# The product PA of the state space on GpSimd, its fin sums with it, and a small copy on ScalarE

## The chip, the cores and the metric

The kernel runs on one core of a Trainium2 chip. The metric is the device time of one execution in microseconds; three executions of the kernel before took 2797.89, 2802.87 and 2807.26 us, so its median is 2802.87. The engines are TensorE (PE in the rows, PEld its weight loads), VectorE (DVE), ScalarE (ACT), GpSimd (POOL) and the queue that issues the transfers (SP).

## The reference, cut to what matters

The reference is one step of a two-layer backbone: attention and an MLP in layer 0, a bidirectional S5 (a state space with 64 groups of 16 channels and a complex diagonal state of 64) with a GLU and an MLP in layer 1. The change touches the state space alone:

```python
def _ssm_scan(u, lam_re, lam_im, log_dt, b_re, b_im, s0_re, s0_im, reverse):
    ...
    bu_re = jnp.einsum('blgc,gpc->blgp', u, bb_re)
    bu_im = jnp.einsum('blgc,gpc->blgp', u, bb_im)
    ...
    _, _, s_re, s_im = lax.associative_scan(_complex_affine_combine, (a_re, a_im, bu_re, bu_im), axis=1)
    ...

def _bidir_s5(h, s0, lam_re, ..., d_skip, w_a, w_b):
    ...
    for d in range(2):
        s_re, s_im = _ssm_scan(u, ..., reverse=(d == 1))
        y = (y + jnp.einsum('blgp,gcp->blgc', s_re, c_re[d])
             - jnp.einsum('blgp,gcp->blgc', s_im, c_im[d]))
        states.append((s_re, s_im))
    y = jax.nn.gelu(y.reshape(b, l, D_MODEL).astype(h.dtype))
    return (y @ w_a) * jax.nn.sigmoid(y @ w_b), states
```

The last states of the context tokens are an output of their own.

## The kernel before, in words

The state space (function s5) works on chunks of 8 tokens: 145 columns stand for the chunks of both streams and a gap between them. The 64 groups go in 16 batches of GB = 4; the partitions hold the 64 states of the forward scan (lo) and the 64 of the backward scan (hi). A complex scan becomes two real ones, one for the real and one for the imaginary part (k = 0, 1), since each state is turned by its angle before the scan and turned back after it; D holds the cosines and sines of the turns.

For one batch b the steps are these:
- v_mm: 32 small products on TensorE write V in PSUM, one buffer (L1068).
- scan(b): ScalarE makes the decay factors `at` (L1078) and copies the initial states into W (L1081); GpSimd clears one column of W (L1082). VectorE turns V: four products of D, in SBUF, with V, in PSUM, into W and t (L1087, L1089), which are called rotations below, then a sum and a difference of W and t, both in SBUF (L1092), called the two sums. It copies the initial states of the backward scan into one column of W (L1094) and runs two scans over `at` and W into Zs (L1098). ScalarE copies Zs into Z, the backward half reversed (L1101, L1102), and GpSimd clears one column of Z (L1103).
- states(b): VectorE turns back: PA, the product of the cosines and Z for both parts at once, 2 x 4 x 146 elements per partition (L1112), and PB, the product of the sines and Z with a sign, in two instructions (L1114). Two sums of 4-element columns of PA and PB give `fin`, the last states (L1117).
- t_mm and y_mm: TensorE adds what the chunk gives to itself (L1127) and 32 products of PA and PB with the matrices ex (L1137) in PSUM; ScalarE copies the sum out (L1140).
- out_y, after each second batch: transfers rearrange the result, and ScalarE makes the GELU (L1153).

W, t, Zs, Z, PA and PB have one buffer each, `at` has two. The loop calls scan(b), then v_mm and t_mm for batch b + 1, then states(b - 1) and y_mm(b - 1). All waits are set by the framework, which also orders each engine's instructions: by the order of the program as priority, among those whose inputs and buffers are ready in its own model of time. So the order on an engine is fixed when the kernel is built and isn't that of the program: in the trace PA of batch b - 1 stands between the sums and the scans of batch b.

In the first batches GpSimd also forms the products of x and rb for the inputs u (L1034 in load_u), from which ScalarE makes hs (L1038). Behind the state space come the splits of y and of the GLU's weights (L52) and the GLU's matmuls.

Of the kernel before, what the change touches and what calls it, by code (L numbers as in the profile page):

```python
# [13 lines left out]
ALU = mybir.AluOpType  # L14
# [5 lines left out]
D = 1024  # L20
# [13 lines left out]
class Body:  # L34
# [746 lines left out]
    NT = 147  # L781
# [119 lines left out]
    GB = 4  # L901
# [100 lines left out]
    def s5(self):  # L1002
        if isinstance(self.YD, int):
            self.YD = YS[self.YD]; self.UD = YS[self.UD]
        nc, tc, a, GB, ND, NT = self.nc, self.tc, self.a, self.GB, self.NT, self.NT - 1
        v, gp, act = nc.vector, nc.gpsimd, nc.scalar
# [11 lines left out]
        with ExitStack() as c2:  # L1018
# [51 lines left out]
                               start=q % 2 == 0, stop=q % 2 == 1, skip_group_check=True)  # L1070
                return V

            def scan(b, V, D):

                gsl = slice(GB * b, GB * b + GB)
                at = S.tile([128, GB, NT], F32, name="at", tag="at", bufs=2)
                for q in range(GB):
                    act.activation(at[:, q, :], am[:, 0:NT], AF.Copy, scale=self.zs[:, GB * b + q, 2:3])  # L1078
                W = S.tile([128, 2, GB, NT], F32, name="W", tag="W", bufs=1)
                zin = self.zs[:, gsl, 0:2].rearrange("p g k -> p k g")  # L1080
                act.copy(W[lo, :, :, 0], zin[lo])  # L1081
                gp.memset(W[hi, :, :, 0:1], 0.0)  # L1082
                t = S.tile([128, 2, GB, 145], F32, name="t", tag="t", bufs=1)
                for k in range(2):
                    vk = [V[:, j, :, 0:290].rearrange("p a (g k) -> p a g k", k=145) for j in (k, 1 - k)]
                    d = [D[:, :, j, 2:147].rearrange("p (a g) k -> p a g k", a=2) for j in range(2)]
                    v.tensor_tensor(out=W[:, k, :, 1:146].rearrange("p (a g) k -> p a g k", a=2), in0=d[0],  # L1087
                                    in1=vk[0], op=ALU.mult)
                    v.tensor_tensor(out=t[:, k].rearrange("p (a g) k -> p a g k", a=2), in0=d[1], in1=vk[1],  # L1089
                                    op=ALU.mult)  # L1090
                for k in range(2):
                    v.tensor_tensor(out=W[:, k, :, 1:146], in0=W[:, k, :, 1:146], in1=t[:, k],  # L1092
                                    op=ALU.add if k == 0 else ALU.subtract)
                v.tensor_copy(W[hi, :, :, 17], zin[hi])  # L1094
                Zs = S.tile([128, 2, GB, NT], F32, name="Zs", tag="Zs", bufs=1)
                for k in range(2):
                    af, wf, zf = (z.rearrange("p g i -> p (g i)") for z in (at, W[:, k], Zs[:, k]))
                    v.tensor_tensor_scan(out=zf, data0=af, data1=wf, initial=0.0, op0=ALU.mult, op1=ALU.add)  # L1098
                Z = S.tile([128, 2, GB, NT], F32, name="Z", tag="Z", bufs=1)
                with self.tc.high_priority(offset=self.HZ):  # L1100
                    act.copy(Z[hi, :, :, 0:145], Zs[hi, :, :, 144::-1])  # L1101
                    act.copy(Z[lo], Zs[lo])  # L1102
                gp.memset(Z[hi, :, :, 145:146], 0.0)  # L1103
                return Z

            def states(b, Z, D):

                gsl = slice(GB * b, GB * b + GB)
                PA = S.tile([128, 2, GB, NT], F32, name="PA", tag="PA", bufs=1)
                PB = S.tile([128, 2, GB, NT], F32, name="PB", tag="PB", bufs=1)  # L1110
                d_r, d_i = D[:, :, 0, 1:147], D[:, :, 1, 1:147]
                v.tensor_tensor(out=PA, in0=d_r[:, None].to_broadcast([128, 2, GB, NT]), in1=Z, op=ALU.mult)  # L1112
                for k in range(2):
                    v.scalar_tensor_tensor(out=PB[:, k], in0=d_i, scalar=am[:, NT + k:NT + k + 1], in1=Z[:, 1 - k],  # L1114
                                           op0=ALU.mult, op1=ALU.mult)
                for r, c in ((lo, 145), (hi, 128)):
                    v.tensor_tensor(out=self.fin[r, :, gsl], in0=PA[r, :, :, c], in1=PB[r, :, :, c], op=ALU.add)  # L1117
                return PA, PB

            def t_mm(b, u, bt):  # L1120

                out = []
                for g in range(0, GB, 2):
                    yp = ps.tile([128, 512], F32, name="yp", tag="y", bufs=2) if b % 2 == 0 else self.bank("yp")
                    out.append(yp)
                    for q in (g, g + 1):
                        mm(yp[:, 145 * (q - g):145 * (q - g) + 145], bt[:, q, 256:384], u[:, GB * (b % 2) + q, :],  # L1127
                           start=q == g, stop=False, skip_group_check=True)
                return out

            def y_mm(b, yps, ex, PA, PB, y8):
                for g, yp in zip(range(0, GB, 2), yps):
                    for q in (g, g + 1):
                        o = yp[:, 145 * (q - g):145 * (q - g) + 145]
                        for k in range(2):
                            for P in (PA, PB):
                                mm(o, ex[:, q, k, :], P[:, k, q, 0:145], start=False, stop=k == 1 and P is PB,  # L1137
                                   skip_group_check=True)
                    gq = GB * (b % 2) + g
                    act.copy(y8[:, gq:gq + 2, :], yp[:, 0:290].rearrange("p (g k) -> p g k", k=145))  # L1140
# [20 lines left out]
            for b in range(nb + 1):  # L1161
                if b < nb:
                    if b == 0:
                        us[1] = load_u(1)
                    if b % 2 == self.LU and (b + self.LU) // 2 + 1 < KT and b:
                        with self.tc.high_priority(offset=self.HU):
                            us[(b + self.LU) // 2 + 1] = load_u((b + self.LU) // 2 + 1)
                    if b + 1 < nb:
                        with self.tc.high_priority(offset=self.HT):
                            tb[b + 1] = load_t(b + 1)  # L1170
                    Zs[b] = scan(b, Vs.pop(b), tb[b][1])
                    if b + 1 < nb:
                        Vs[b + 1] = v_mm(b + 1, us[(b + 1) // 2], tb[b + 1][0])
                        Ts[b + 1] = t_mm(b + 1, us[(b + 1) // 2], tb[b + 1][0])
                if b > 0:
                    c = b - 1
                    if c % 2 == 0:
                        y8 = S.tile([128, 8, 145], F32, name="y8", tag="y8", bufs=1)
                    y_mm(c, Ts.pop(c), tb[c][2], *states(c, Zs.pop(c), tb[c][1]), y8)
                    if c == nb - 1:  # L1180
                        self.gw0 = [self.glu_w(k, 0) for k in range(2)]
                    if c % 2 == 1:
                        out_y(c // 2, y8)
# [216 lines left out]
```

## Time and profile before

| | before |
|---|---|
| three executions, median | 2802.87 us |
| the profiled execution, its own time | 2799.74 us |
| its span, first to last instruction | 2797.8 us |
| mean granted TensorE clock | 0.979 of 2.4 GHz |
| busy: TensorE, VectorE, ScalarE, GpSimd | 93%, 65%, 39%, 13% of the span |
| the state space | about 1568 to 1745 us |

The profile is one execution, read by the chip's profiler. Shares of busy time are means over stages with different limits, so a stage has to be cut out to see what bounds it there. A row of the timeline gives the start, the duration, the engine, the line, the operation, what it writes and reads, the shape and how many instructions are merged in it; in brackets stands the idle time of the engine ahead of it and what ended that. VectorE's records overlap a little: the distance between two starts is what an instruction costs the queue.

### The profile page before, as it was taken

What the parts mean: (1) busy time and instruction counts of PE and PEld (TensorE: products, weight loads), DVE (VectorE), ACT (ScalarE), POOL (GpSimd) and SP (SyncE); (2) the same over time, 40 slices, a digit from 0 to 9 for tenths busy, and PEclk for the clock granted to TensorE, in tenths of its full rate; (3) what the DMA queues carried; (4) which work ended last, traced back from release to release, by engine and by line L of the source; (5) the groups of instructions that cost most, each with busy time, mean ns of one, the idle gap of its engine ahead of it and who ended that gap; (6) DMA issues with size and microseconds to landing.
All of it is one profiled execution on the core that took longest, in us unless ns stands there. A gap on an engine that the chain in (4) does not pass through costs nothing. (4 is left out here: it accounts for less than half of the span.)

```text
span 2797.8 us, 44016 instructions
## 1 busy us (share of the span) xinstructions
PE 2609.5 (93%) x16561; PEld 2462.1 (88%) x16561; DVE 1824.4 (65%) x4342; ACT 1096.1 (39%) x2295; POOL 366.6 (13%) x476
## 2 busy tenths in 40 slices
PE   6889999998899999999899687999999999999997
PEld 4767987886699989899899676999999999999997
DVE  4847777785576787887875799545645354454455
ACT  3545666662223323332333655434422222212224
POOL 1222222210022132121220400000000000000002
PEclk8999999999999999999999799999999999999998
DMA  7353222235532233132223586433110111111101
GB/s 264 109 169 105 84 79 74 81 116 189 180 103 75 70 95 90 55 105 71 88 83 91 174 251 180 141 121 113 46 46 31 46 46 46 34 43 46 46 31 68
DMA packets 128452, 271.67 MB, mean 97 GB/s; under 512 B 13296, under 2 KB 67952, under 8 KB 126832
## 3 DMA queue, kind: packets, MB, share of 16 engines
q1 hardware_dynamic: 128240, 268.86, 30.3%
q8 instruction: 131, 2.15, 0.3%
q14 instruction: 81, 0.66, 0.1%
HBM read 214.22 MB, written 39.81 MB: 91 GB/s over the span
## 5 line engine op out<-in xcount | busy, mean ns | idle before, releaser
L455 DVE SCALAR_TENSOR_TENSOR x<-m,mod,x 128x384 f32<-128x384 f32 (+2 forms) x1024 | 496.2, 512 | 149.2 <-PE m L47 145.3
L47 PE MATMUL m<-at,w 128*128 128x384 f32 x1536 | 523.4, 341 | 0.0
L45 PE MATMUL m<-at,w 128*128 128x384 f32 x1536 | 522.7, 340 | 0.8 <-DVE x L455 0.8
L46 PE MATMUL m<-at,w 128*128 128x384 f32 x1536 | 521.7, 340 | 0.0
L45 PE MATMUL m<-mh,w 128*128 128x384 f32 x1024 | 349.1, 342 | 1.9 <-ACT mh L237 1.9
L47 PE MATMUL m<-mh,w 128*128 128x384 f32 x1024 | 349.9, 342 | 0.0
L46 PE MATMUL m<-mh,w 128*128 128x384 f32 x1024 | 349.8, 342 | 0.0
L52 DVE TENSOR_TENSOR at<-r,at 128x384 fp32r<-128x384 f32 x192 | 111.6, 583 | 361.4 <-ACT at L51 361.2
L51 ACT CAST w<-wr 128x1024 fp32r<-128x1024 f32 x128 | 131.0, 1046 | 524.4 <-PE m L46 515.7
L47 PEld LDWEIGHTS m<-at,w 128*128 128x128 f32 x1536 | 289.1, 188 | 9.2 <-issue 8.9
L45 PEld LDWEIGHTS m<-at,w 128*128 128x128 f32 x1536 | 289.2, 188 | 3.8 <-issue 1.8
L46 PEld LDWEIGHTS m<-at,w 128*128 128x128 f32 x1536 | 289.1, 188 | 2.8 <-issue 2.5
L683 ACT ACTIVATE r<-m 128x384 f32<-128x384 f32 x192 | 93.8, 490 | 373.1 <-PE m L47 370.3
L45 PEld LDWEIGHTS m<-mh,w 128*128 128x128 f32 x1024 | 193.9, 190 | 7.4 <-issue 4.8
L52 DVE TENSOR_TENSOR w<-wr,w 128x1024 fp32r<-128x1024 f32 x128 | 156.6, 1243 | 64.9 <-ACT w L51 60.6
L47 PEld LDWEIGHTS m<-mh,w 128*128 128x128 f32 x1024 | 194.5, 190 | 3.6 <-issue 3.5
L46 PEld LDWEIGHTS m<-mh,w 128*128 128x128 f32 x1024 | 194.4, 190 | 1.6 <-issue 0.8
L45 PE MATMUL m<-h,w 128*128 128x384 f32 x512 | 174.4, 341 | 1.5 <-ACT w L51 0.7
L47 PE MATMUL m<-h,w 128*128 128x384 f32 x512 | 173.9, 340 | 1.2 <-DVE w L52 1.2
L46 PE MATMUL m<-h,w 128*128 128x384 f32 x512 | 174.5, 341 | 0.0
L1242 POOL TENSOR_TENSOR fo<-fo,rb 128x384 f32<-128x384 f32 x18 | 20.6, 1176 | 1034.7 <-ACT rb L224 1026.9
L389 POOL TENSOR_SCALAR pt<-pt,sst 128x512 f32<-128x512 f32 (+1 forms) x144 | 102.6, 724 | 298.4 <-DVE sst L387 153.8
(328 smaller groups left out, 5161.1 us busy)
## 6 DMA issues: line engine op xcount, KB each, us to landing
wr<-in_w_dram SPq DMA_DIRECT2D x128, 512.0 KB, 4.4
wm<-in_w_mod_dram SPq DMA_DIRECT2D x80, 512.0 KB, 4.6
wr<-in_glu_dram SPq DMA_DIRECT2D x48, 512.0 KB, 3.3
wr<-in_w_qo_dram SPq DMA_DIRECT2D x24, 512.0 KB, 3.3
wr<-in_w_qo_dram SPq DMA_DIRECT2D x48, 256.0 KB, 2.8
bt<-bt_d SPq DMA_DIRECT2D x16, 768.0 KB, 5.5
dt_d<-d SPq DMA_DIRECT2D x32, 294.0 KB, 2.1
D<-dt_d SPq DMA_DIRECT2D x16, 588.0 KB, 4.7
```

Of the source, the lines that this page charges most:

```text
L45: mm(out, lh, rh, start=first, stop=False)
L46: mm(out, lh, rl, start=False, stop=False)
L47: mm(out, ll, rh, start=False, stop=last)
L51: (ceng.copy if ceng is self.nc.scalar else ceng.tensor_copy)(h, src)
L52: seng.tensor_tensor(out=l, in0=src, in1=h, op=ALU.subtract)
L389: nc.gpsimd.tensor_scalar(p[:, e, :nk], p[:, e, :nk], rc[:, e:e + 1], 1.0, op0=ALU.mult, op1=ALU.mult)
L455: nc.vector.scalar_tensor_tensor(out=self.x[c][:, m, lo:hi], in0=ps[:, lo:hi], scalar=self.gate(layer, j, m, s), in1=self.x[c][:, m, lo:hi ...
L683: nc.scalar.activation(r, pt[:, :CW], AF.Relu)
L1242: nc.gpsimd.tensor_tensor(out=z, in0=z, in1=self.rb[c], op=ALU.mult)
```

## The change

scan is cut into turn (everything up to the last write of W) and scan proper. PA and the two fin sums go from VectorE to GpSimd; the copy into column 17 of W goes from VectorE to ScalarE. In the loop states(b - 1) is now called between turn(b) and scan(b), and for the last batch in an iteration of its own; y_mm takes its result. No tile, buffer count or transfer changes.

```diff
--- before.py
+++ after.py
@@ -1070,7 +1070,7 @@
                                start=q % 2 == 0, stop=q % 2 == 1, skip_group_check=True)
                 return V
 
-            def scan(b, V, D):
+            def turn(b, V, D):
 
                 gsl = slice(GB * b, GB * b + GB)
                 at = S.tile([128, GB, NT], F32, name="at", tag="at", bufs=2)
@@ -1091,7 +1091,11 @@
                 for k in range(2):
                     v.tensor_tensor(out=W[:, k, :, 1:146], in0=W[:, k, :, 1:146], in1=t[:, k],
                                     op=ALU.add if k == 0 else ALU.subtract)
-                v.tensor_copy(W[hi, :, :, 17], zin[hi])
+                act.copy(W[hi, :, :, 17], zin[hi])
+                return at, W
+
+            def scan(at, W):
+
                 Zs = S.tile([128, 2, GB, NT], F32, name="Zs", tag="Zs", bufs=1)
                 for k in range(2):
                     af, wf, zf = (z.rearrange("p g i -> p (g i)") for z in (at, W[:, k], Zs[:, k]))
@@ -1109,12 +1113,12 @@
                 PA = S.tile([128, 2, GB, NT], F32, name="PA", tag="PA", bufs=1)
                 PB = S.tile([128, 2, GB, NT], F32, name="PB", tag="PB", bufs=1)
                 d_r, d_i = D[:, :, 0, 1:147], D[:, :, 1, 1:147]
-                v.tensor_tensor(out=PA, in0=d_r[:, None].to_broadcast([128, 2, GB, NT]), in1=Z, op=ALU.mult)
+                gp.tensor_tensor(out=PA, in0=d_r[:, None].to_broadcast([128, 2, GB, NT]), in1=Z, op=ALU.mult)
                 for k in range(2):
                     v.scalar_tensor_tensor(out=PB[:, k], in0=d_i, scalar=am[:, NT + k:NT + k + 1], in1=Z[:, 1 - k],
                                            op0=ALU.mult, op1=ALU.mult)
                 for r, c in ((lo, 145), (hi, 128)):
-                    v.tensor_tensor(out=self.fin[r, :, gsl], in0=PA[r, :, :, c], in1=PB[r, :, :, c], op=ALU.add)
+                    gp.tensor_tensor(out=self.fin[r, :, gsl], in0=PA[r, :, :, c], in1=PB[r, :, :, c], op=ALU.add)
                 return PA, PB
 
             def t_mm(b, u, bt):
@@ -1168,15 +1172,21 @@
                     if b + 1 < nb:
                         with self.tc.high_priority(offset=self.HT):
                             tb[b + 1] = load_t(b + 1)
-                    Zs[b] = scan(b, Vs.pop(b), tb[b][1])
+                    w = turn(b, Vs.pop(b), tb[b][1])
+
+                    if b > 0:
+                        P = states(b - 1, Zs.pop(b - 1), tb[b - 1][1])
+                    Zs[b] = scan(*w)
                     if b + 1 < nb:
                         Vs[b + 1] = v_mm(b + 1, us[(b + 1) // 2], tb[b + 1][0])
                         Ts[b + 1] = t_mm(b + 1, us[(b + 1) // 2], tb[b + 1][0])
+                else:
+                    P = states(b - 1, Zs.pop(b - 1), tb[b - 1][1])
                 if b > 0:
                     c = b - 1
                     if c % 2 == 0:
                         y8 = S.tile([128, 8, 145], F32, name="y8", tag="y8", bufs=1)
-                    y_mm(c, Ts.pop(c), tb[c][2], *states(c, Zs.pop(c), tb[c][1]), y8)
+                    y_mm(c, Ts.pop(c), tb[c][2], *P, y8)
                     if c == nb - 1:
                         self.gw0 = [self.glu_w(k, 0) for k in range(2)]
                     if c % 2 == 1:
```

## Rows read from the trace of the kernel before

**Rows 1.** The page, part 1: busy us (share of the span) and instructions of each engine

```profile
PE 2609.5 (93%) x16561; PEld 2462.1 (88%) x16561; DVE 1824.4 (65%) x4342; ACT 1096.1 (39%) x2295; POOL 366.6 (13%) x476
```

**Rows 2.** Windows: us; PE, PEld, DVE, ACT, POOL busy; PEclk, DMA, GB/s. Batches 1, 5, 7

```profile
1578.40:1590.00 11.60, 5.84 (x44) 5.24 (x44) 11.13 (x12) 6.50 (x12) 5.08 (x5) 0.71 0.49 160
...
1623.20:1635.40 12.20, 11.69 (x82) 11.10 (x82) 9.95 (x15) 5.21 (x12) 0.21 (x2) 0.74 0.81 261
...
1655.40:1665.40 10.00, 7.94 (x72) 7.05 (x72) 9.91 (x15) 6.67 (x11) 0.21 (x2) 1.00 0.88 281
```

**Rows 3.** Timeline of VectorE over one steady batch

```profile
1656.03 0.75 DVE L1087 TENSOR_TENSOR W<-D,V 128x580 f32<-128x580 f32 x1
1656.69 0.34 DVE L1117 TENSOR_TENSOR fin<-PA,PB 64x8 f32<-64x8 f32 x2
1657.05 0.76 DVE L1089 TENSOR_TENSOR t<-D,V 128x580 f32<-128x580 f32 x1
...
1659.06 1.43 DVE L1092 TENSOR_TENSOR W<-W,t 128x580 f32<-128x580 f32 x2
1660.41 1.37 DVE L1112 TENSOR_TENSOR PA<-D,Z 128x1168 f32<-128x1168 f32 x1
1661.81 0.17 DVE L1094 COPY W<-zs 64x8 f32<-64x8 f32 x1
1662.01 0.82 DVE L1114 SCALAR_TENSOR_TENSOR PB<-D,am,Z 128x584 f32<-128x584 f32 x1
1662.76 2.63 DVE L1098 TENSOR_TENSOR_SCAN Zs<-at,W 128x584 f32<-128x584 f32 x2
1665.31 0.80 DVE L1114 SCALAR_TENSOR_TENSOR PB<-D,am,Z 128x584 f32<-128x584 f32 x1
1666.03 0.75 DVE L1087 TENSOR_TENSOR W<-D,V 128x580 f32<-128x580 f32 x1
```

**Rows 4.** The chain that ended last, around the last batch: start, us, what

```profile
1732.72 2.63 DVE Zs L1098 x2
...
1740.33 4.47 PE yp L1137 x32
```

**Rows 5.** Lines L52 and L1034, GpSimd's products: duration ns min/median/max

```profile
L52 POOL TENSOR_TENSOR wv<-wr,wv x2: 2388/2540/2692, 50.3 to 52.7; 128x1024 fp32r<-128x1024 f32 x2
L1034 POOL TENSOR_TENSOR nt<-x,rb x21: 987/1003/2063, 1555.8 to 1604.8; 128x384 f32<-128x384 f32 x21
```

**Rows 6.** Timelines of VectorE and GpSimd, batches 0 to 3

```profile
1574.33 4.04 DVE L1098 TENSOR_TENSOR_SCAN Zs<-at,W 128x584 f32<-128x584 f32 x2
...
1601.48 1.49 DVE L1114 SCALAR_TENSOR_TENSOR PB<-D,am,Z 128x584 f32<-128x584 f32 x1
1602.89 0.75 DVE L1087 TENSOR_TENSOR W<-D,V 128x580 f32<-128x580 f32 x1
...
1596.76 8.99 POOL L1034 TENSOR_TENSOR nt<-x,rb 128x384 f32<-128x384 f32 x6 [5.88 <-ACT hs L1038]
```

**Rows 7.** Timelines of GpSimd and VectorE, the start of the kernel

```profile
36.46 2.58 POOL L52 TENSOR_TENSOR wk<-wr,wk 128x1024 fp32r<-128x1024 f32 x1 [36.02 <-ACT wk L51]
...
36.74 3.38 DVE L52 TENSOR_TENSOR wk<-wr,wk 128x1024 fp32r<-128x1024 f32 x1
```

**Rows 8.** Timelines of ScalarE and VectorE behind the scans of batch 0

```profile
1578.40 1.16 ACT L1101 COPY Z<-Zs 64x1160 f32<-64x1160 f32 x1 [3.01 <-DVE Zs L1098]
1579.58 1.17 ACT L1102 COPY Z<-Zs 64x1168 f32<-64x1168 f32 x1
...
1578.81 0.76 DVE L1087 TENSOR_TENSOR W<-D,V 128x580 f32<-128x580 f32 x1 [0.44 <-issue]
```

**Rows 9.** Timelines of ScalarE and VectorE behind the scans of the last batch

```profile
1737.35 1.17 ACT L1102 COPY Z<-Zs 64x1168 f32<-64x1168 f32 x1
...
1736.83 1.23 DVE L52 TENSOR_TENSOR gw<-wr,gw 128x1024 fp32r<-128x1024 f32 x1
...
1740.19 1.56 DVE L1114 SCALAR_TENSOR_TENSOR PB<-D,am,Z 128x584 f32<-128x584 f32 x2
```

**Rows 10.** Waits in the state space: us in total, times, longest

```profile
DVE PA L1112 <- PE yp L1137: 2.2, 1, 2.2
```

## The prediction

> **What bounds the kernel now.** I read the page first: TensorE is busy for 93% of the span [rows 1], so almost everywhere another engine's work is worth nothing. Then I cut the state space (1568 to 1745 us) into its batches, from the end of one pair of scans to the end of the next [rows 2]. There VectorE is busy for 9.91 of 10.00 us per batch and GpSimd for 0.21; TensorE has gaps. This is the one stretch in which VectorE sets the pace, and it is what the change works on. The three rows stand for all: batches 1 to 3 take 11.6 us each, batch 4 takes 10.0, batch 5 takes 12.2, and batches 6 to 15 take 10.0 each. VectorE's own timeline gives the cycle of a steady batch [rows 3]; the time from one start to the next is what an instruction costs the queue. Four rotations (L1087, L1089) take 0.67 us each, 2.68 together; two sums (L1092) 1.35; PA 1.40; the small copy into W 0.20; the two PB 0.74 and 0.72; two scans 2.55; the two fin 0.36. The sum is 10.0. What comes behind the state space waits for its last batch, as the chain shows [rows 4], so its delay reaches the end in full.
>
> **What is removed.** PA, the W copy and the fin leave VectorE: 1.40 + 0.20 + 0.36 = 1.96 us per batch, 16 batches. Without any new wait a cycle would take 8.04 us.
>
> **What is added on GpSimd.** PA has 1168 elements per partition. GpSimd's products of two float32 inputs took 1.00 us for 384 elements and 2.54 us for 1024 (median, 2.39 to 2.69) [rows 5]. By the element that is 2.33 to 2.63 ns, so PA is 2.7 to 3.1 us; I take 2.9, from the longer instruction, which is nearer in size. That is twice what it cost VectorE, which would not matter if it ran beside it. The Trainium skill (GPSIMD Engine Reference, Elementwise — side-by-side cycle accounting) has 4497 ns for 2048 elements; by it PA would be about 2.6 us, an estimate, and each cycle below 0.3 us shorter; the rows of this trace are dearer, and the sum goes by them.
>
> **Does it run beside VectorE?** The rows of batches 0 to 3, where GpSimd works on L1034, say when [rows 6]. A rotation, whose second input is in PSUM, took its usual 0.75 us at 1602.89 with GpSimd busy. A PB took 1.49 instead of 0.80 us, a pair of scans 4.04 instead of 2.63 us: instructions with both inputs in SBUF stand still until GpSimd's instruction is over, and GpSimd's own took up to 2.06 instead of 1.00 us [rows 5]. It is an exclusion, not a sharing, and it holds for long instructions too: a VectorE difference over 1024 elements took 3.38 us behind a GpSimd product of 2.58 us [rows 7]. The Trainium skill says the same of the pair of ports that the two engines share (SBUF — State Buffer, Who interferes with whom): the later one is blocked for the other's whole instruction. By that rule PA is covered by rotations alone, and the trace agrees.
>
> So of a cycle only the 2.68 us of rotations can hide PA. But PA needs Z, and Z comes from ScalarE: two copies of 1.16 and 1.17 us behind the scans [rows 8]. At 1578.40 the first began 0.03 us after the scans' end; so Z is there 2.4 us after the scans at the best, and the rotations of the next batch, which need neither, start at once or up to 0.44 us later (that is what it took at 1578.81, where no PB stood in between). PA therefore meets only the last 0.3 us of the rotations and then holds up the two sums, which are next in VectorE's queue.
>
> **The new cycle,** from the end of the scans: Z 2.4, PA 2.9, sums 1.35, PB 1.46, scans 2.55, together 10.66. The two fin are queued on GpSimd behind PA and wait for PB; the first will be asked for while the first scan runs, and gets its turn before the second: I put 0.15 us, from 0.15 to 0.18 us that a fin took on VectorE [rows 3] (bounds 0 and 0.3). Some 0.1 us for the handovers between engines (the gap at 1578.40, three or four times). That is 10.9, against 10.0: **+0.9 us per batch**. If Z is late, because ScalarE is in a GELU, the first sum goes ahead of PA and the rest waits; the exclusion still costs nearly the whole 2.9, at 8.04 + 2.9 + 0.15 and up to 0.3 more: 11.35. With PA at 2.7 and no handovers it is 10.6. Bounds +0.6 and +1.35.
>
> The W copy on ScalarE has the sums ahead of it and the scans behind it. It takes 0.2 us, and 1.46 us of PB on VectorE cover it; only behind a GELU would it show, and then the sums, too, are late. I put it at nothing; without the cover it would be 0.3 us a batch. Behind the waiting fin stand only memsets of Z and W and, early on, L1034, whose results are wanted batches later.
>
> **The sum.** Batch 4 and batches 6 to 15: 11 x 0.9 = 9.9 (6.6 to 14.9). Batches 1 to 3, where L1034 already costs 1.6 us of each 11.6 and PA comes on top of a busier ScalarE: 1.2 each, 3.6 (1.5 to 9). Batch 5 lost 2.2 us waiting for TensorE before PA [rows 10]; with longer cycles part of that is slack: -0.3 (-1.3 to +1). The tail: from the end of the last scans (1735.35) to the end of the last products (1744.80) it is 9.45 us [rows 4]. After the change Z is ready at 2.4 instead of 3.2 [rows 9], since no PB of the batch before holds it; PA 2.9, PB 1.5, the products behind the last PB 3.05 (from 1741.75), and half of a split of 1.23 us [rows 9] that may have the ports when PA comes: 10.45, +1.0 (0 to 2.3). Together 9.9 + 3.6 - 0.3 + 1.0 = **+14.2 us** (6.8 to 27). The profiled execution took 2799.7 us (span 2797.8); it would take 2813.9. That execution is 3.1 us under the median of the runs, 2802.9, which would become **2817**.
>
> **The rivals.** *PA is hidden after all:* GpSimd's 2.9 us lie beside work that does not need the shared ports, and VectorE keeps most of its 1.96 us. It would need Z at the start of the rotations, or PA given out a batch late; then a cycle is at best 8.04 + 0.2 for what sticks out + 0.15, and 15 cycles of 1.6 us less give 24 us: 2779. It decides as soon as PA meets over 1.8 us of the rotations. Rows 6 and 7 speak against the first half, rows 8 against the second; 8%. *Blocked, but given back:* the cycle stays at 10.6, batch 5's stall goes, and the early batches lose little because ScalarE and not VectorE sets them: +3, within 0 to 8, 2806; 20%. *TensorE becomes the bound:* the products of a batch now start only behind the later PB, about 8.1 us into the cycle, and need 3.05 us; that ends 0.3 us into the next cycle, ahead of PA at 2.4. In batches 1 and 5 the granted clock was 0.71 and 0.74 [rows 2], partly at the lower of its two levels (1.2 of 2.4 GHz); there the products take twice as long and end at 3.3 us, and PA, which writes what they read, waits for them: 0.9 us, or up to the 2.2 us of batch 5. TensorE's longer gaps make this likelier; 1 to 2 us more in eight batches give 2829; 12%. *The change doesn't do what it says* is my forecast in a way: PA lies beside the sums, not the rotations.
>
> **How the numbers follow.** My forecast has 60%, 2817, its own range 2809 to 2830. About 0.3% (8.4 us) is what a measurement of this kernel can tell from no change. Faster: the first rival, 8%. Within 0.3% (2794.5 to 2811.3): the second rival and a small part of the forecast's low end, 24%. Slower: 68%. The range leaves out the first rival and the farthest of the third: 2803 to 2836.
>
> **What would show it.** In the steady batches VectorE's timeline should show the first or second sum at about 2.9 to 3.5 instead of 0.75 us, GpSimd's PA at 2.7 to 3.1 us, beginning 2.4 us behind the scans, and cycles of 10.6 to 11.4 us; VectorE's summed busy time should not fall, although its instructions are fewer. Sums of 0.75 us with PA running would disprove the exclusion; a PA that begins together with the rotations would make the first rival right; idle time before PA that ends with L1137 would make it the third; cycles under 10 us would make the forecast wrong.

## The result, and the profile after

| | before | after |
|---|---|---|
| time, median of four executions | 2802.48 us (2797.89 to 2807.26) | 2824.68 us (2824.17 to 2825.48) |
| profiled execution: time, span | 2799.7, 2797.8 us | 2825.5, 2823.6 us |
| end of the first scans to end of the last, 15 cycles | 1578.4 to 1735.4 | 1579.3 to 1753.8 |
| one undisturbed cycle | 10.00 us | 10.54 us |

The change makes the kernel slower: the ratio is 1.0078, with a 95% interval of 1.0064 to 1.0091, about +22 us. By spans it is 25.8 us, since the profiled execution of before lies 3 us under its median and that of after 1 us over its own. The table that follows adds up the spans.

The page of after, part 1 (busy us, share of the span, instructions); it answers to [rows 1]:

```profile
PE 2621.7 (93%) x16561; PEld 2474.9 (88%) x16561; DVE 1830.5 (65%) x4278; ACT 1097.6 (39%) x2311; POOL 443.6 (16%) x524
```

VectorE has 64 instructions fewer than in [rows 1] and is busy 6 us longer. Where that time went stands in the groups by line. Here is the line of the two sums over the state space, in before and in after, and behind them that of PA in before (count, busy us, mean ns of one, idle time before them and what ended it):

```profile
L1092 DVE TENSOR_TENSOR W<-W,t 128x580 f32<-128x580 f32 x32 | 23.8, 784 | 0.0
```

```profile
L1092 DVE TENSOR_TENSOR W<-W,t 128x580 f32<-128x580 f32 x32 | 48.6, 1557 | 0.0
```

```profile
L1112 DVE TENSOR_TENSOR PA<-D,Z 128x1168 f32<-128x1168 f32 x16 | 21.9, 1368 | 2.2 <-PE yp L1137 2.2
```

The same 32 sums take twice as long: 24.8 us more, against the 21.9 us that PA's sixteen products had cost VectorE. The timelines of VectorE, GpSimd and ScalarE in one undisturbed batch show how (start, us, engine, line; the scans before it end at 1637.74):

```profile
1637.83 0.76 DVE L1087 TENSOR_TENSOR W<-D,V 128x580 f32<-128x580 f32 x1
...
1640.51 3.74 DVE L1092 TENSOR_TENSOR W<-W,t 128x580 f32<-128x580 f32 x2
1644.18 1.55 DVE L1118 SCALAR_TENSOR_TENSOR PB<-D,am,Z 128x584 f32<-128x584 f32 x2
1645.65 2.62 DVE L1102 TENSOR_TENSOR_SCAN Zs<-at,W 128x584 f32<-128x584 f32 x2
```

```profile
1640.30 2.66 POOL L1116 TENSOR_TENSOR PA<-D,Z 128x1168 f32<-128x1168 f32 x1 [2.34 <-ACT Z L1106]
1645.87 2.41 POOL L1121 TENSOR_TENSOR fin<-PA,PB 64x8 f32<-64x8 f32 x2 [2.91 <-DVE PB L1118]
```

```profile
1637.83 1.16 ACT L1105 COPY Z<-Zs 64x1160 f32<-64x1160 f32 x1 [2.52 <-POOL Z L1107]
1639.00 1.17 ACT L1106 COPY Z<-Zs 64x1168 f32<-64x1168 f32 x1
```

The rotations run from 1637.83 to 1640.5, and in that time ScalarE makes Z. PA starts at 1640.30, when they are nearly over; the sums, which took 1.43 us in [rows 3], stand at 3.74. PA lies beside the sums and not beside the rotations.

Not all batches are like that one. The cycles, from the end of one pair of scans to the end of the next, worked out from the scans' ends in the traces:

```
batch    1    2    3    4    5    6    7    8    9    10   11   12   13   14   15
before  11.6 11.6 11.6 10.0 12.2 10.0 10.0 10.0 10.0 10.0 10.0 10.0 10.0 10.0 10.0
after   12.0 12.7 12.5 10.5 10.7 10.5 11.9 10.6 10.5 12.7 10.5 14.0 10.5 13.8 10.9
```

Set against the sum of the prediction:

| part | forecast, us | by the spans, us |
|---|---|---|
| up to the end of batch 0 | 0 | +0.9 |
| batches 1 to 3 | +3.6 | +2.4 |
| batch 5 | -0.3 | -1.5 |
| batch 4 and 6 to 15, undisturbed cycle | +9.9 (11 x 0.9) | +5.9 (11 x 0.54) |
| the same batches, what is over 10.54 | 0 | +10.6 |
| tail, last scans to last product | +1.0 | +4.1 |
| behind the state space | 0 | +3.3 |
| sum | +14 | +25.7 |

The forecast was 2817 us, the time is 2825. The undisturbed cycle was dearer in the forecast than on the chip, and something that its sum did not have costs 10.6 us in single batches: 1.3 us in batch 7, where a GELU stands between the two copies of Z, 2.1, 3.5 and 3.3 in 10, 12 and 14, and 0.4 in the others. Here is batch 12, in the timelines of ScalarE, TensorE and VectorE:

```profile
1695.22 1.17 ACT L1106 COPY Z<-Zs 64x1168 f32<-64x1168 f32 x1
...
1697.02 2.23 ACT L1157 ACTIVATE yh<-yt 128x1024 f32<-128x1024 f32 x2
1699.16 1.26 ACT L1144 COPY y<-yp 128x290 f32<-128x290 f32 x4
```

```profile
1694.53 0.41 PE L1141 MATMUL yp<-PB,ex 128*128 128x145 f32 x2
1699.59 4.24 PE L1131 MATMUL yp<-u,bt 128*128 128x145 f32 x16 [4.65 <-ACT y L1144]
...
1706.45 2.19 PE L1068 MATMUL V<-u,bt 128*64 128x145 f32 x32
```

```profile
1708.70 0.76 DVE L1087 TENSOR_TENSOR W<-D,V 128x580 f32<-128x580 f32 x1 [4.20 <-PE V L1068]
```

The y products end at 1694.9. Their results leave PSUM only at 1699.16, as ScalarE has the copies of Z, two of `at` and a GELU ahead of the y copies. The t products (L1131), which need their banks, wait 4.65 us for that and then take 4.24 us at a granted clock of 0.50. V, which has a buffer of its own, stands behind them and behind nine y products in TensorE's queue, and the rotations, which could have begun at 1704.5 behind the scans, wait 4.20 us for V. Batch 10 has the same picture with a wait of 2.14 us. In batch 14 a split of y stands ahead of the rotations in VectorE's queue and waits 4.49 us for ScalarE, so the profile has no wait for V there; but V, behind eight t products that had waited 4.97 us for y copies, ends only 0.3 us before the split begins:

```profile
1731.08 2.20 PE L1068 MATMUL V<-u,bt 128*64 128x145 f32 x32
```

```profile
1733.57 0.56 DVE L52 TENSOR_TENSOR ys<-yh,ys 128x384 fp32r<-128x384 f32 x1 [4.49 <-ACT ys L51]
```

In the program, where each engine's order is fixed when the kernel is built, TensorE's sequence in the second half is this (V16 are the sixteen V products of a batch, t4 its four t products, y16 its y products; the trace counts each of them twice; the end of the state space is to the right):

```
before        ... y16 V16 y6 t4 y9 t2 y1 V3 t2 V13 y16 V16 y6 t4 y8 t2 y2 V3 t2 V13 y16 V16 y7 t4 y7 t2 y2 t2 y32
after         ... V16 y16 V16 y16 t8 y2 V16 y14 V16 y16 t8 y9 V16 y9 V16 y14 t8 y10 V16 y8 V16 y14 t8 y32
```

In after, eight t products of two batches stand together, and a V behind them. Whether this order is the cause, or only the place where a delay of other origin shows, is what the second set of experiments asks.

### The profile page after: what moved, and what is told of

It reads as the page before. It is cut to its first block, busy times and chain, and to the rows that moved or that the text cites. A ratio compares the mean times of both kernels' runs of the same rounds, so it can differ in the third digit from the quotient of the medians.

```text
span 2823.6 us, 44041 instructions
## 1 busy us (share of the span) xinstructions
PE 2621.7 (93%) x16561; PEld 2474.9 (88%) x16561; DVE 1830.5 (65%) x4278; ACT 1097.6 (39%) x2311; POOL 443.6 (16%) x524
## 5 line engine op out<-in xcount | busy, mean ns | idle before, releaser
L52 DVE TENSOR_TENSOR at<-r,at 128x384 fp32r<-128x384 f32 x192 | 111.7, 584 | 360.7 <-ACT at L51 360.4
L52 DVE TENSOR_TENSOR w<-wr,w 128x1024 fp32r<-128x1024 f32 x128 | 156.8, 1244 | 66.3 <-ACT w L51 62.0
```

The costliest lines, as they stand in the source:

```text
L52: seng.tensor_tensor(out=l, in0=src, in1=h, op=ALU.subtract)
```

## Experiments on the cycle

Ratios are against the kernel before, from runs beside it, with 95% intervals.

**The parts one by one.** pa_on_vector is the changed kernel with PA back on VectorE:

```diff
-                gp.tensor_tensor(out=PA, in0=d_r[...], in1=Z, op=ALU.mult)
+                v.tensor_tensor(out=PA, in0=d_r[...], in1=Z, op=ALU.mult)
```

> The changed kernel with PA given back to VectorE; order of the steps, fin on GpSimd and the W copy on ScalarE stay as changed. Theory of the shared ports: PA on GpSimd is what lengthens the cycle, because the sums stand still behind it. With PA on VectorE an undisturbed cycle is 2.68 + 1.35 + 1.40 + 1.47 + 2.55 + 0.1 = 9.55 us instead of 10.55, so 15 us less, 2810. If the late products on TensorE (waits of 2 to 4.5 us before the rotations in every second late batch) also come from PA's lateness, they go too: 2798 to 2802. Rival, the new order of the steps costs the time, whatever engine makes PA: 2815 or more.

2798.3 us, ratio 0.9985 (0.9971 to 1.0000). The undisturbed cycle is 9.5 us:

```profile
1662.70:1672.20 9.50, 8.64 (x82) 7.86 (x80) 9.41 (x12) 4.46 (x11) 2.58 (x4) 1.00 0.84 280
```

That line is a window over one batch (columns as in [rows 2]). Everything that the change loses goes with this one edit: PA on GpSimd costs 26 us in the setting of the new order. Whether 2 us more are gained against the kernel before is open, since the interval touches 1.

pa_only is the opposite, the kernel before with PA alone moved:

```diff
-                v.tensor_tensor(out=PA, in0=d_r[...], in1=Z, op=ALU.mult)
+                gp.tensor_tensor(out=PA, in0=d_r[...], in1=Z, op=ALU.mult)
```

> The kernel before with PA alone on GpSimd; order of the steps, fin and the W copy as before. Theory of the shared ports: VectorE gives up 1.40 us and stands still for up to 2.67 us per batch, less what rotations cover: a cycle of 10.7 to 11.3 instead of 10.0, 2813 to 2830, with products of TensorE coming late as in the changed kernel. Rival, the order costs the time: 2806 or less.

2830.0 us, ratio 1.0099 (1.0066 to 1.0131), undisturbed cycle 10.9 us, disturbed ones 12.2 to 13.8. The cost of PA does not come from the new order of the code. TensorE's sequence in this kernel is that of after, product for product, so the order on TensorE, too, comes with PA on GpSimd.

order_only has the new order alone, with PA, the W copy and the fin all on VectorE:

```diff
-                act.copy(W[hi, :, :, 17], zin[hi])
+                v.tensor_copy(W[hi, :, :, 17], zin[hi])
...
-                gp.tensor_tensor(out=PA, ...)
+                v.tensor_tensor(out=PA, ...)
...
-                    gp.tensor_tensor(out=self.fin[r, :, gsl], ...)
+                    v.tensor_tensor(out=self.fin[r, :, gsl], ...)
```

> The kernel before with the new order of the steps alone (turn, then states of the batch before, then scan); every operation on the engine it had before. Theory of the shared ports: no GpSimd work, so VectorE's cycle is the old sum, 10.0 to 10.1 us, and the time is within 6 us of before: 2799 to 2808. Rival, the order costs the time: 2815 or more.

2808.5 us, ratio 1.0025 (1.0012 to 1.0039): a little slower, and just over the band. Its undisturbed cycle is 10.2, since the first rotation now stands directly behind the second scan and starts 1.46 us after the scan's start, where in before the next instruction started after 1.27; single cycles take 10.6 to 12.3 us in the second half, and why is not shown.

small_only is the kernel before with the W copy on ScalarE and the fin on GpSimd:

```diff
-                v.tensor_copy(W[hi, :, :, 17], zin[hi])
+                act.copy(W[hi, :, :, 17], zin[hi])
...
-                    v.tensor_tensor(out=self.fin[r, :, gsl], ...)
+                    gp.tensor_tensor(out=self.fin[r, :, gsl], ...)
```

> The kernel before with its order of the steps and PA on VectorE; only the two fin go to GpSimd and the W copy to ScalarE. If what VectorE gives up (0.56 us per batch) is gained one for one, the cycle is 9.45 instead of 10.0: 2791 to 2796. Rival, the W copy on ScalarE comes late or the fin on GpSimd hold up the scans: no gain, 2799 or more.

2806.8 us, ratio 1.0008 (0.9992 to 1.0024): no gain, where 2791 to 2796 was expected. From batch 4 on every second cycle is 9.3 us, about what the instructions removed would give, and those between them are 10.1 to 11.2. VectorE's waits in the state space say why (us in total, times, longest):

```profile
DVE Zs L1098 <- ACT W L1094: 4.4, 4, 2.4
DVE PA L1112 <- PE yp L1137: 4.2, 3, 1.8
DVE PA L1112 <- ACT Z L1102: 2.6, 2, 1.3
DVE PA L1112 <- ACT W L1094: 1.8, 1, 1.8
DVE PA L1112 <- ACT y L1140: 1.3, 1, 1.3
```

The first row is the W copy: in batches 0 to 3 the scans wait for it, 4.4 us in all. The other rows are PA, which stands ahead of the scans and starts 0.6 to 1.8 us late in batch 2 and in every second batch from 5 on. PA does not read W; by the timelines it starts each time within 0.1 to 0.2 us of the end of the copies of Z, which stand behind a GELU on ScalarE, or of the y products that read its tile. So most of what the shorter cycles give is lost to PA's waits, and a part to the W copy. A copy that VectorE makes in 0.2 us is not free on an engine that is asked for it at one moment and is busy then.

**Is it exclusion?** pa_twice forms PA a second time, into the same tile:

```diff
                 gp.tensor_tensor(out=PA, in0=d_r[...], in1=Z, op=ALU.mult)
+                gp.tensor_tensor(out=PA, in0=d_r[...], in1=Z, op=ALU.mult)
```

> The changed kernel with PA formed twice by GpSimd, one instruction behind the other, into the same tile. Theory of the shared ports: the second stands in VectorE's way for its whole 2.66 us as well; undisturbed cycles of 13.2 instead of 10.55 us, 40 us in all, 2858 to 2868. If the sums and PB slip in between and what is late is only PA itself, the cycle grows by less, 2845 or less.

2851.3 us, ratio 1.016 (1.0137 to 1.0183); the median is 7 us below the band. VectorE's sums and GpSimd's two products in an undisturbed batch:

```profile
1651.41 6.22 DVE L1092 TENSOR_TENSOR W<-W,t 128x580 f32<-128x580 f32 x2
```

```profile
1651.22 2.67 POOL L1116 TENSOR_TENSOR PA<-D,Z 128x1168 f32<-128x1168 f32 x1 [2.36 <-PE yp L1142]
1653.96 3.04 POOL L1117 TENSOR_TENSOR PA<-D,Z 128x1168 f32<-128x1168 f32 x1
```

The engines alternate: PA, a sum, PA, a sum. Each PA lengthens the sums by most of its own time, 2.3 and 2.5 us (1.43, 3.74, 6.22), and the undisturbed cycle is 13.0 to 13.2 us, as expected to 0.2. The total rose less, by 27 us instead of 40: what single batches take over the undisturbed cycle falls from 10.6 us in after to 4.4 here.

**Beside the rotations.** z_by_part copies Z half by half and gives PA to GpSimd in halves, so that the first can start when half of Z is there:

```diff
-                    act.copy(Z[hi, :, :, 0:145], Zs[hi, :, :, 144::-1])
-                    act.copy(Z[lo], Zs[lo])
+                    for k in range(2):
+                        act.copy(Z[hi, k, :, 0:145], Zs[hi, k, :, 144::-1])
+                        act.copy(Z[lo, k], Zs[lo, k])
...
-                gp.tensor_tensor(out=PA, in0=d_r[...], in1=Z, op=ALU.mult)
+                for k in range(2):
+                    gp.tensor_tensor(out=PA[:, k], in0=d_r, in1=Z[:, k], op=ALU.mult)
```

> The changed kernel with Z copied part by part (real, then imaginary, 64 x 584 each) and PA on GpSimd in two instructions, one per part. The copies of the first part can run beside the second scan, so PA's first half can begin about when the rotations do, and its second half 1.3 us later. Theory of the shared ports: both halves now lie beside the rotations, the sums are not held up any more, and an undisturbed cycle falls from 10.55 to 8.2 to 9.0 us (the transfers, 0.87 busy at 10 us a batch, allow little under 9): 2785 to 2805. Rival, PA on GpSimd is dear wherever it lies, or the order costs the time: 2818 or more.

2809.5 us, ratio 1.003 (1.0015 to 1.0044): missed, although the mechanism works. GpSimd and VectorE in one batch:

```profile
1641.28 1.43 POOL L1118 TENSOR_TENSOR PA<-D,Z 128x584 f32<-128x584 f32 x1 [0.21 <-POOL W L1082]
1644.95 1.42 POOL L1118 TENSOR_TENSOR PA<-D,Z 128x584 f32<-128x584 f32 x1 [2.25 <-ACT Z L1107]
```

```profile
1641.32 0.75 DVE L1089 TENSOR_TENSOR t<-D,V 128x580 f32<-128x580 f32 x1
...
1643.33 1.43 DVE L1092 TENSOR_TENSOR W<-W,t 128x580 f32<-128x580 f32 x2
1644.96 2.77 DVE L1120 SCALAR_TENSOR_TENSOR PB<-D,am,Z 128x584 f32<-128x584 f32 x2 [0.21 <-issue]
```

The first half of PA lies beside two rotations; neither is longer than alone, and the sums stay at 1.43. The second meets PB, which goes from 1.56 to 2.77. Cycles of 8.8 to 9.2 us are there, four of fifteen; the others are 9.7 to 14.9, with the same waits as in after (t products for y copies 15.6 us in all, V 4.9 us, between 1640 and 1740).

half_y8 takes what is free of this: Z copied half by half as there, the first half of PA on GpSimd beside the rotations, the second on VectorE, and a second buffer for y8 (paid for by one buffer of `at`, and by letting the fin share another tile):

```diff
+                for k in range(2):
+                    (gp if k == 0 else v).tensor_tensor(out=PA[:, k], in0=d_r, in1=Z[:, k], op=ALU.mult)
...
-                        y8 = S.tile([128, 8, 145], F32, name="y8", tag="y8", bufs=1)
+                        y8 = S.tile([128, 8, 145], F32, name="y8", tag="y8", bufs=2)
```

> The changed kernel with Z copied part by part, the real part of PA on GpSimd, the imaginary part on VectorE, and two buffers for y8 (made room for as in the other kernel). GpSimd's half takes 1.4 us and can start 0.1 us behind the scans, so all of it lies beside the rotations (2.68 us). Theory of the shared ports: nothing stands still; VectorE's sum is 2.68 + 1.35 + 0.70 + 1.47 + 2.55 + 0.1 = 8.85 us per batch, and with the transfers 9.0 to 9.4: 2780 to 2790, faster than both. Rival, GpSimd beside VectorE is dear wherever it lies: 2798 or more.

2792.3 us, ratio 0.9958 (0.9943 to 0.9973): 2 us over what was expected, by its median the fastest of all kernels here, and faster than both the kernel before and the changed one. Seven cycles in a row are 8.9 us. One batch of it in VectorE's and GpSimd's timelines:

```profile
1648.16 0.75 DVE L1089 TENSOR_TENSOR t<-D,V 128x580 f32<-128x580 f32 x1
...
1650.16 1.43 DVE L1092 TENSOR_TENSOR W<-W,t 128x580 f32<-128x580 f32 x2
1651.51 0.76 DVE L1118 TENSOR_TENSOR PA<-D,Z 128x584 f32<-128x584 f32 x1
```

```profile
1648.25 1.42 POOL L1118 TENSOR_TENSOR PA<-D,Z 128x584 f32<-128x584 f32 x1 [0.63 <-PE yp L1143]
```

## Experiments on the disturbed batches

**Buffers.** after_y8 is the changed kernel with two buffers for y8, in case the y copies wait for the one that the former pair of batches still holds:

```diff
-                        y8 = S.tile([128, 8, 145], F32, name="y8", tag="y8", bufs=1)
+                        y8 = S.tile([128, 8, 145], F32, name="y8", tag="y8", bufs=2)
```

> The changed kernel with two buffers for y8, the result of two batches (room for it: the decay factors get one buffer instead of two, and fin shares the buffer of the initial states, which are no longer needed). With one buffer all four copies of y stand behind a GELU on ScalarE, TensorE waits for them, and the products V of a later batch behind that make VectorE wait. Theory of the y copies: the waits before the rotations (2.1, 4.2, 4.5 us) go, undisturbed cycles stay at 10.55: 15 cycles take about 164 instead of 174.5 us, 2811 to 2817. Rival, V is late because PA on GpSimd and the lower clock make the products late in any order: 2821 or more.

2825.4 us, ratio 1.0067 (1.0043 to 1.0091): that theory fell. The y copies come in pairs and singly instead of in fours, but cycles of 14.7, 13.6 and 15.8 us are still there.

pav_y8 is pa_on_vector with the same second buffer; its order on TensorE comes out the same in every batch:

```
pav_y8        V16 t8 V32 y16 t4 V16 y16 t4 V16 y16 t4 ... V16 y16 t4 V16 y16 t4 y32
```

> The changed kernel with PA back on VectorE (as in pa_on_vector, 2798 us) and with two buffers for y8; the W copy and the last sum of the scans stay off VectorE, the order stays the new one. TensorE's fixed order is then the same in every batch: sixteen V, sixteen y products, four t products. Theory A (irregular cycles come from that order): every cycle after the first three is 9.5 to 9.8 us, median 2790 to 2797 us. Theory B (the order does not matter where VectorE has slack): some cycles of 10.5 us and more stay, and it is 2797 us or more, as pa_on_vector.

2798.5 us, ratio 0.9982 (0.9967 to 0.9997), the time of pa_on_vector, and from batch 1 on the same cycles to 0.1 us. A regular order alone brings nothing where V was not late.

**V ahead by priority.** after_y8_v200 and half_y8_v200 give V a higher priority when the order is made:

```diff
-                        Vs[b + 1] = v_mm(b + 1, us[(b + 1) // 2], tb[b + 1][0])
+                        with self.tc.high_priority(offset=200):
+                            Vs[b + 1] = v_mm(b + 1, us[(b + 1) // 2], tb[b + 1][0])
```

> The kernel after_y8 (the changed kernel with two buffers for y8), with one more edit: the sixteen products V of the next batch are given priority, so that in TensorE's order, fixed when the program is built, all sixteen stand ahead of most of the t and y products from the ninth batch on too, where after_y8 had them behind. Theory A (the late batches wait because V stands in that order behind products that PA, PB or a y copy make late): VectorE no longer stands still at the rotations for V (after_y8: 15.5 us in that group), the late cycles of 13.6 to 15.8 us go down to 10.5 to 11.5, and the median is 2808 to 2818 us. Theory B (the waits come from the late products themselves, at TensorE's lower clock, wherever V stands): the wait moves from V to PA or to the y products, cycles of over 12.5 us stay, and the median is 2821 us or more.

> The kernel half_y8 (Z copied by part, the real half of PA on GpSimd, the imaginary on VectorE, two buffers for y8; 2792 us with cycles of 8.9 and some of 10.6 to 11.6), with the sixteen products V of the next batch given priority in TensorE's order. Theory A: its late cycles of 10.6 and 11.6 us go to 9.2 or less, 2785 to 2791 us. Theory B: they stay or others take their place, 2791 to 2800 us.

2826.6 us, ratio 1.0088 (1.0061 to 1.0115), and 2803.3 us, ratio 0.9997 (0.9983 to 1.0011). Both missed: half_y8_v200 is 11 us slower than half_y8. By the numbers this would be theory B, but the program shows that the edit did not do what it was for. The order of after_y8_v200 in the second half is

```
after_y8_v200 ... y13 V16 t2 y3 t2 y2 V16 y14 t4 y13 V16 t2 y3 t2 y2 V16 y14 t4 y14 V16 t2 y2 t2 y2 V16 y14 t4 ...
```

with every second V behind t products that wait for y copies of the products just ahead of them. So these two runs tell nothing on the theories. In the trace VectorE's wait for V is longer, 25.9 us in six places against the 15.5 us in four of after_y8, but that is an execution of 2836 us, 10 us over the median.

**V ahead by hand.** after_y8_vo writes the order out: t is formed one batch later, and t and y are queued behind the V of the next batch.

```diff
+                            last = mm(V[...])
...
-                        Ts[b + 1] = t_mm(b + 1, us[(b + 1) // 2], tb[b + 1][0])
+                    if b > 0:
+                        with self.tc.issue_after(self.vlast):
+                            Ts[b] = t_mm(b, us[b // 2], tb[b][0])
...
-                    y_mm(c, Ts.pop(c), tb[c][2], *P, y8)
+                    with self.tc.issue_after(self.vlast):
+                        y_mm(c, Ts.pop(c), tb[c][2], *P, y8)
```

```
after_y8_vo   V16 t4 V32 t4 y16 V16 t4 y16 V16 t4 y16 ... V16 t4 y16 V16 t4 y16 t4 y32
```

> The kernel after_y8 (the changed kernel with two buffers for y8, 2825.4 us) with TensorE's order written out by hand, and nothing else: the t products of a batch are formed one batch later, and the t and y products stand behind the sixteen products V of the next batch. In every batch the order is then V, t, y; no V stands behind a t product that waits for a y copy on ScalarE, as it does from the ninth batch on in the changed kernel (t8 y9 V16). (In after_y8_v200 the priority moved V, but two of three V still stood behind t products.) Theory A (the late batches wait because V stands behind t products, these wait for y copies, and the y copies stand behind GELU on ScalarE): no wait of VectorE for V after the first batches, every cycle from the fourth on 10.5 to 10.9 us, and the median is 2806 to 2815 us. Theory B (the late products and the lower clock themselves hold up the batches, wherever V stands): cycles of over 12.5 us stay in the second half, GpSimd waits for the y products to free PA, and the median is 2819 us or more.

2815.9 us, ratio 1.0040 (1.0026 to 1.0054); the interval of the changed kernel, 1.0064 to 1.0091, lies wholly above it. That of after_y8, from which it differs by the order alone, overlaps it at the edge (from 1.0043), but the slowest execution of after_y8_vo, 2817.2, is faster than the fastest of after_y8, 2821.1. The waits of VectorE for V in the state space (us in total, times, longest), in after_y8 and after_y8_vo:

```profile
DVE W L1087 <- PE V L1068: 15.5, 4, 8.2
```

```profile
DVE W L1088 <- PE V L1068: 8.2, 1, 8.2
```

The one of 8.2 us is ahead of batch 0 and is in both. The others are gone, and the cycles are these:

```
after_y8      12.0 12.7 12.5 10.9 10.5 10.8 10.5 11.4 10.5 14.7 10.7 13.6 10.5 15.8 10.5
after_y8_vo   12.0 14.0 12.3 10.5 10.7 10.5 10.7 11.0 10.5 11.0 10.6 10.7 10.6 11.7 10.6
```

From batch 4 on the sum falls from 140.6 to 129.1 us. One cycle, 11.7, is over the band, two of 11.0 touch it, and the median is 1 us above it. In batches 8 and 10, the two of 11.0, the scans wait some 0.3 us for the W copy and a PB slips between them. In batch 14, the one of 11.7, PA waits until the y products that read its tile are over, 3.1 us behind Z, and meets a scan and PB, with a split and a short wait for the W copy ahead of it. In batch 11 GpSimd's timeline shows PA waiting in the same way and meeting PB instead of the sums:

```profile
1699.63 2.87 POOL L1117 TENSOR_TENSOR PA<-D,Z 128x1168 f32<-128x1168 f32 x1 [3.48 <-PE yp L1142]
```

This costs only 0.1 us there (10.6), since the wait lies beside the rotations and the sums, and VectorE then stands behind PA as long as it would have otherwise.

Over the undisturbed 10.54, batches 4 and 6 to 15 have 2.5 us left of the 10.6 in after. So the order on TensorE, in which V stands behind t products that wait, accounts for some 8 us of them. That ScalarE's GELU ahead of the y copies begins it, the other half of theory A, was seen in the timelines only and not tried by itself.

## Why the prediction was right, point by point

**The whole: right in direction and mechanism, near in size partly by luck.** Of the 25.7 us in the table, the terms that the forecast's sum named (the cycle, the early batches, batch 5 and the tail) have 10.9, where it had 14.2. The other 14.8 are waits in single batches and two stretches for which the sum had nothing; terms that were too dear made up for a part of them.

**What bounds the kernel: right.** VectorE paces the state space in after too: its instructions fill 10.45 of 10.56 us of the undisturbed batch, 2.3 of them standing behind PA. The lines are windows over that batch and over the last products:

```profile
1637.74:1648.30 10.56, 6.94 (x66) 6.07 (x66) 10.45 (x10) 3.87 (x8) 5.19 (x7) 1.00 0.77 246
1760.67:1767.03 6.36, 6.36 (x31) 6.36 (x31) 2.38 (x3) 0.88 (x3) 1.26 (x2) 0.57 0.27 93
```

**PA meets the sums: right.** Z is ready 2.43 us behind the scans and PA starts at 2.56 (forecast 2.4 and a handover), and the two sums take 3.74 us together, the first about 3.1 of it, within the 2.9 to 3.5 named. pa_twice shows the exclusion, z_by_part and half_y8 that rotations cover GpSimd's work at no cost. The Trainium skill (SBUF — State Buffer, Who interferes with whom) says the same: with two inputs in SBUF an instruction of VectorE contends with a GpSimd instruction that reads SBUF; with at most one, and outside the modes that use two ports, it does not. The trace agrees on both sides, 3.74 against 1.43 us and 0.75 against 0.75.

**The terms of the cycle: right in kind, 0.4 us too dear.** PA measured 2.66 us in place of 2.9, just under the bounds of 2.7 to 3.1: that is 2.28 ns by the element, less than either product of [rows 5]. It lies nearer to the estimate from the Trainium skill (GPSIMD Engine Reference, Elementwise — side-by-side cycle accounting), about 2.6 us; here the trace agrees with the page. The fin, put at 0.15, cost nothing: they stand on GpSimd for 2.41 us, each until a scan ends, but the two scans take 2.62, as before. Sums behind PA took 1.22 instead of 1.35. That makes 10.54 instead of 10.9, +0.54 us per batch against +0.9, and 4 us less over eleven batches. The case of a late Z behind a GELU, put at 11.35 (its terms add up to 11.39), came once, in batch 7, and took 11.9: PB, too, waited 1.05 us for Z.

**The waits: the step that failed.** The prediction had TensorE only as a rival, by way of the y products that PA must wait for, at 1 to 2 us in eight batches; its sum had no wait for TensorE in the late batches. There after loses 2.1 to 3.5 us each in batches 10, 12 and 14, 8.9 us together. PA does show the rival's sign in them: it starts 5.7 to 6.1 us behind the scans instead of 2.56, when the y products end. But VectorE stood still before that, 2.14 and 4.20 us for V in 10 and 12, and in 14 for 4.49 us at a split with V ready only shortly before. V was late through an order that was made anew when the program was built. The text treated the order of TensorE and ScalarE as unchanged and looked only at what each instruction waits for. after_y8_vo shows that the order carries most of it. With V ahead 2816 us remain; that this is close to the forecast is partly chance, since in its trace the cycle is cheaper than in the sum, the tail (+2.1) is dearer, and 3.2 us more than in before lie ahead of the first rotation, where the change does nothing.

**The W copy "at nothing": wrong in places.** In batch 0 of after it shows, in ScalarE's and VectorE's timelines:

```profile
1574.15 1.20 ACT L1038 ACTIVATE hs<-nt,mod,gs 128x256 f32<-128x256 f32 x2 [0.42 <-POOL nt L1034]
1575.37 0.20 ACT L1094 COPY W<-zs 64x8 f32<-64x8 f32 x1
```

```profile
1575.67 3.60 DVE L1102 TENSOR_TENSOR_SCAN Zs<-at,W 128x584 f32<-128x584 f32 x2 [2.41 <-ACT W L1094]
```

The scans wait 2.41 us, and batch 0 takes 11.1 us from its first rotation to the end of its scans instead of 10.1. It takes 11.1 to 11.2 in all eleven kernels here with the copy on ScalarE, and 10.1 to 10.2 in the three without (before, pa_only, order_only). The cover named was PB, but batch 0 has no PB of a batch before it. In small_only, without PA's delay as a cover, the scans wait for the copy in batches 1 to 3 too, for 2.0 us.

**The tail: +4.1 instead of +1.0, and over its bound of 2.3.** The prediction had half a split ahead of PA; PA came first and held a split up, for 2.70 us instead of 0.55, and PB stood 0.8 us behind PA for it and for one more:

```profile
1756.34 2.65 POOL L1116 TENSOR_TENSOR PA<-D,Z 128x1168 f32<-128x1168 f32 x1 [2.51 <-ACT Z L1106]
```

```profile
1756.71 2.70 DVE L52 TENSOR_TENSOR ys<-yh,ys 128x384 fp32r<-128x384 f32 x1 [0.88 <-issue]
```

But most is the term for the products behind the last PB. It was taken at 3.05 us, and it took 5.9 us (from 1761.36 to 1767.29): TensorE had waited 3.26 us for PA and 0.97 for PB, and the granted clock of the stretch is 0.57, near the lower of its two levels (1.2 and 2.4 GHz). The prediction had this price in its third rival and did not carry it to the tail.

**Batch 5 and batches 1 to 3: right,** -1.5 (a little beyond its bound of -1.3) and +2.4 (within 1.5 to 9). The 2.2 us of [rows 10] are gone.

**Behind the state space: +3.3 us, left open.** In after the GLU has one stretch more at the lower clock (0.85 in the window 1974 to 2008). From the last split of y to the end it takes 1045.8 us in after and 1042.2 in before. The profiled executions of all kernels here fall into two groups: 1045.8 to 1047.0 in after, pa_on_vector, order_only, pav_y8 and half_y8, 1042.0 to 1042.9 in the others. PA is on GpSimd in pa_only, pa_twice and after_y8, which are in the second group, and on VectorE in order_only, which is in the first. So it isn't PA; what calls it forth was not tried.

**Of the rivals** "PA is hidden after all" fell as the change stands. half_y8 hides half of PA; its point of decision, over 1.8 us of PA beside the rotations, is not reached, and it gains 0.4%. "Blocked, but given back" would have needed a loss of 0 to 8 us; the interval of the ratio excludes it.

## What to carry to other kernels

Before an operation goes to GpSimd, look at which of VectorE's instructions will stand beside it at the moment when its input is ready: those that read PSUM cover it, those with both inputs in SBUF are put off until it is over, so a product that takes twice as long there can cost more than it takes away. Move as much as fits beside the former (here half of PA), and start it early by splitting what feeds it. And a moved operation changes the order in which the program is built on all engines; compare the order of the engine that is close to its limit, and write it out by hand where what the bounding engine needs next stands behind work that waits.

## What the runs showed of the hardware

- Between a VectorE instruction with both inputs in SBUF and a GpSimd product the exclusion goes by whole instructions: with two PA in a row the sums stood at 6.22 us for 1.35 us of work. It held for sums of 0.75 us behind PA of 2.66 us, and for PA, which took 3.04 us where it came behind a sum. Rotations, with one input in PSUM, kept their 0.75 us beside GpSimd.
- It costs the two sides differently when one is small: a fin, 0.21 us on GpSimd where VectorE stood idle, took up to 1.2 us beside the scans, and the scans stayed at 2.62 us.
- TensorE's idle time had a price after it. In after the eight t products took 4.24 us behind a gap of 4.65 us, all of them at the lower clock (0.50 in the first row below). In after_y8_vo, behind V without a gap and at the full clock (1.00 in the window 1704.82 to 1706.08), four took 1.26 us, so eight would take 2.5, an estimate:

```profile
1699.59:1703.83 4.24, 4.24 (x17) 4.24 (x18) 4.24 (x6) 1.76 (x6) 1.67 (x2) 0.50 0.21 48
```

```profile
1704.82 1.26 PE L1132 MATMUL yp<-u,bt 128*128 128x145 f32 x8
```
